# Gate products in pieces of twelve in every second step of a round, in place of six in every step

## The chip, the cores and the metric

The kernel runs on one core of one Trainium2 chip. The metric is the device time of one execution in microseconds (us); the median of the runs shown is used.

## The reference, cut to what matters

The program computes one layer of a hybrid encoder for 2048 frames of width 1024, all in float32:

```python
h = rmsnorm(x)
proj = h @ w_in                       # u | rwkv_in | gate_a | gate_b
o_a = s5_branch(u)                    # diagonal state space model
o_b = rwkv7_branch(rwkv_in)           # 8 heads x 64, delta rule over time
merged = sigmoid(gate_a) * (o_a @ wb[:512]) + sigmoid(gate_b) * (o_b @ wb[512:])
x = x + merged @ w_out
x = x + relu(rmsnorm(x) @ w_ff1)**2 @ w_ff2
return rmsnorm(x)
```

The change concerns the gate columns of `h @ w_in` (2048 columns, here called the gate products) and the RWKV recurrence, since both are computed in the same stage.

## The kernel before, in words

There are four stages. Stage A normalises x, computes the first part of the input projection and the state space branch. Stage B (`phase_b`) runs the RWKV recurrence and, beside it, all the gate products. Stage C merges the branches and applies `w_out`; stage D is the feed-forward part. This case is about stage B.

**The gate products** are made by the generator `gates` (from L957). The outer loop runs over four windows `w` of 512 frames, the inner one over 16 column blocks `m` of 128. One tile `gp` (128 columns by 512 frames, one PSUM bank, two banks in turn) takes eight blocks k of the contraction, and each block takes three TensorE products (`mm3`, L120 to L123: high part by low part, low by high, high by high). So a tile is 24 products of 128x128 by 128x512, and there are 64 tiles and 1536 products. When a tile is done, ScalarE copies it out of PSUM to `gs` (L1015) and a DMA on SP's queue stores it in `gt_d` one tile later (L1016, through `late`). At the start of a tile `loadw` (L965 on) asks for the next block's weights: in the first window ScalarE and GpSimd split raw weights into high and low part (L976, L977), later the parts are read back from `gs_d` (L972). Two weight slots exist, one for even and one for odd m. At the start of each window eight tiles `gh` of the normalised input are loaded from `h_d`, and five steps pass without a product.

**The recurrence** is worked in 16 blocks of 128 frames. For each block there are three generators: `elem` (element-wise preparation, with the products `n` and `bo`), `inv` (the products `m`, `vt`, `kb`, `mv`, a small triangular inverse on VectorE at L813 and L815 that goes through memory by `inv_d` and comes back as `X`, then the products `P`, `D`, `P`, `D` in `levels`), and `chain` (the carried state: product `R`, VectorE add `Rs` at L903, product `U`, ScalarE copy `VU` at L909, products `S` and `y`, VectorE update `SB` at L928; twice per block, then the output norm with the products `var` and `gt`).

**Rounds and steps.** In round i the function `robin` (L82) takes turns: one step of `chain` for block i-2, one step of `gates`, one step of `elem` for block i, one step of `inv` for block i-1. A step is what a generator does up to its next `yield`. `elem` and `inv` last 15 steps and `chain` 10, so that a full round has 15 steps; `gates` is a side generator that goes on from round to round and is run to its end after the last. Four steps make a tile.

**What sets the order.** Engines execute their instructions strictly in the order of their streams. The order in which the Python code calls the instructions is a priority: a planner builds each engine's stream with estimated durations, and where the instruction that is next by priority is not ready by its estimate it puts a later one there that is ready. Instructions marked with `pin` (the products `m`, `mv`, the first `P` and `D`, and `R`) must stay behind the instruction that was called before them on the same engine. The products of one tile stay in their order.

Of the kernel before, what the change touches and what calls it, by code (L numbers as in the profile page):

```python
# [21 lines left out]
NK = DM // 128  # L22
# [97 lines left out]
def mm3(nc, ps, wh, wl, xh, xl, start, stop):  # L120
    nc.tensor.matmul(ps, wh, xl, start=start, stop=False)  # L121
    nc.tensor.matmul(ps, wl, xh, start=False, stop=False)  # L122
    nc.tensor.matmul(ps, wh, xh, start=False, stop=stop)  # L123
# [487 lines left out]
def phase_b(tc, nc, K, io, pm_d, ob_d, h_d, gt_d, gs_d, inv_d):  # L611
    V, A, P, T = nc.vector, nc.scalar, nc.gpsimd, nc.tensor
    NS = S // 128
    with ExitStack() as st:
# [61 lines left out]
        def pin(f):  # L676
            return lambda *a, **k: tc.keep_in_program_order(f(*a, **k))
# [279 lines left out]
        def gates():  # L957
            late, keep = Late(), Late()

            def raww(m, q=nc.sync):  # L960
                wr = (gw, gt)[m % 2].tile([128, NK, 128], F32, tag="wr", name=f"gwr{m}")
                pin(q.dma_start)(wr, io["win"][18 + m])
                return wr

            def loadw(m, wr=None):  # L965

                pool = (gw, gt)[m % 2]
                wh = pool.tile([128, NK, 128], F32R, tag="wh", name=f"gwh{m}")
                wl = pool.tile([128, NK, 128], F32R, tag="wl", name=f"gwl{m}")
                if m >= 16:  # L970
                    for e, t in enumerate((wh, wl)):
                        nc.sync.dma_start(t.bitcast(F32), gs_d[m % 16, e])  # L972
                    return wh, wl
                if wr is None:
                    wr = raww(m)
                A.copy(wh, wr)  # L976
                P.tensor_tensor(wl, wr, wh, op=ALU.subtract)  # L977

                def store():
                    for e, t in enumerate((wh, wl)):  # L980
                        nc.sync.dma_start(gs_d[m, e], t.bitcast(F32))

                keep.put(store)
                return wh, wl

            wr0 = raww(0, nc.gpsimd)
            yield
            wr1 = raww(1)
            for w in range(NW):
                hs = []  # L990
                for k in range(NK):
                    t = (gw if k < 5 else gt).tile([128, 2, 512], F32R, tag=f"h{k}", name=f"gh{w}_{k}")
                    q = nc.sync if w or k >= 5 else nc.gpsimd
                    (q.dma_start if w else pin(q.dma_start))(
                        t.bitcast(F32), h_d[:, w, :, k, :].rearrange("i p t -> p i t"))
                    r = t[:, 0], t[:, 1]
                    hs.append(r)
                if w == 0:
                    nxt = loadw(0, wr0)
                for _ in range(5):  # L1000
                    yield
                for m in range(16):
                    wh, wl = nxt
                    j = 16 * w + m
                    if j == 15:
                        keep.flush()
                    if j + 1 < 16 * NW:
                        nxt = loadw(j + 1, None if j else wr1)
                    pp = psd.tile([128, 512], F32, tag="d", name=f"gp{j}")
                    for k in range(NK):  # L1010
                        mm3(nc, pp, wh[:, k], wl[:, k], hs[k][0], hs[k][1], k == 0, k == NK - 1)
                        if k % 2 and k < NK - 1:
                            yield
                    sg = gt.tile([128, 512], F32, tag="sg", name=f"gs{j}", bufs=2)
                    A.copy(sg, pp)  # L1015
                    late.put(lambda m=m, w=w, sg=sg: nc.sync.dma_start(  # L1016
                        gt_d[128 * m:128 * m + 128, 512 * w:512 * w + 512], sg))
                    yield
            late.flush()

        gg = Side(gates())
        next(gg)
        load(0, nc.gpsimd)
# [867 lines left out]
```

## Time and profile before

| | |
|---|---|
| median of 3 runs | 3067.3 us (3063.57 to 3067.74) |
| the profiled execution | 3067.71 us, its span 3065.8 us |
| mean granted TensorE clock | 0.975 |
| TensorE busy over the span | 95% |
| VectorE, ScalarE, GpSimd busy | 62%, 37%, 40% |
| stage B's gate products | first start 550.2 us, last 1349.0 us |

Times in the trace are counted from the start of the span. A row of the timeline gives the start, the duration, the engine, the line, what is written from what, and in brackets the idle time of the engine before it with what ended it. Matmuls are pipelined, so the distance between two starts says more than the duration. PE is TensorE, PEld its weight loads, DVE VectorE, ACT ScalarE, POOL GpSimd.

### The profile page before, as it was taken

What the parts mean: (1) busy time and instruction counts of PE and PEld (TensorE: products, weight loads), DVE (VectorE), ACT (ScalarE), POOL (GpSimd) and SP (SyncE); (2) the same over time, 40 slices, a digit from 0 to 9 for tenths busy, and PEclk for the clock granted to TensorE, in tenths of its full rate; (3) what the DMA queues carried; (4) which work ended last, traced back from release to release, by engine and by line L of the source; (5) the groups of instructions that cost most, each with busy time, mean ns of one, the idle gap of its engine ahead of it and who ended that gap; (6) DMA issues with size and microseconds to landing.
All of it is one profiled execution on the core that took longest, in us unless ns stands there. A gap on an engine that the chain in (4) does not pass through costs nothing.

```text
span 3065.8 us, 45565 instructions
## 1 busy us (share of the span) xinstructions
PE 2915.4 (95%) x17024; PEld 2329.5 (76%) x17024; DVE 1897.8 (62%) x3307; ACT 1121.4 (37%) x1797; POOL 1234.7 (40%) x1082
## 2 busy tenths in 40 slices
PE   8989999689999999999999989999999999999998
PEld 6757777467777777777878778887788788888886
DVE  6366885467777677535322376658655476666667
ACT  5342111234333333234444365555433432222232
POOL 3101101754443343113333345555544565555563
PEclk9999999789999999999999999999999999999999
DMA  4344444755656455367665653333533486666664
GB/s 154 96 132 148 132 148 133 255 187 176 187 167 207 120 149 181 118 195 229 194 213 166 192 188 124 110 110 114 169 113 107 134 240 151 151 151 151 153 146 148
DMA packets 328172, 486.04 MB, mean 159 GB/s; under 512 B 112832, under 2 KB 171712, under 8 KB 327952
## 3 DMA queue, kind: packets, MB, share of 16 engines
q1 hardware_dynamic: 298352, 438.08, 44.8%
q0 software_dynamic: 12960, 40.87, 7.3%
q10 hardware_dynamic: 16640, 4.20, 0.5%
q8 instruction: 134, 2.20, 0.3%
q14 instruction: 86, 0.70, 0.1%
HBM read 327.71 MB, written 147.85 MB: 155 GB/s over the span
## 4 chain that ended last, share of the span: by engine, by line
PE 55%; DVE 10%; DMA 6%; issue 4%; POOL 3%; ACT 2%; SPq 1%; POOLq 0%; DVEq 0%; ACTq 0%
PE s L121 6%; PE s L122 6%; PE s L123 6%; PE f L121 6%; PE f L123 6%; PE f L122 6%; PE gp L121 2%; PE gp L122 2%; PE gp L123 2%; DMA g<-gt_d 1%; PE o L121 1%; DVE yt L813 1%; PE o L122 1%; DVE YC L815 1%; PE o L123 1%
## 5 line engine op out<-in xcount | busy, mean ns | idle before, releaser
L121 PE MATMUL f<-bl,w1h 128*128 128x512 f32 x896 | 354.4, 396 | 9.4 <-ACT w1h L1378 9.3
L122 PE MATMUL f<-bh,w1l 128*128 128x512 f32 x896 | 350.7, 391 | 5.1 <-POOL w1l L1382 5.1
L123 PE MATMUL f<-bh,w1h 128*128 128x512 f32 x896 | 352.1, 393 | 0.0
L121 PE MATMUL s<-w2l,ah 128*128 128x512 f32 x784 | 305.8, 390 | 2.9 <-ACT s L1619 2.9
L122 PE MATMUL s<-w2h,al 128*128 128x512 f32 x784 | 305.7, 390 | 0.0
L123 PE MATMUL s<-w2h,ah 128*128 128x512 f32 x784 | 305.6, 390 | 0.0
L1382 POOL TENSOR_TENSOR w1l<-w1r,w1h 128x512 fp32r<-128x512 f32 x122 | 179.9, 1478 | 180.2 <-ACT w1h L1378 179.8
L121 PE MATMUL gp<-gh,gwh 128*128 128x512 f32 x512 | 225.8, 441 | 21.4 <-ACT gwh L976 14.9
L122 PE MATMUL gp<-gh,gwl 128*128 128x512 f32 x512 | 211.6, 413 | 12.5 <-POOL gwl L977 11.7
L1378 ACT CAST w1h<-w1r 128x512 fp32r<-128x512 f32 x224 | 137.9, 620 | 207.9 <-PE f L123 149.7
L1596 POOL TENSOR_TENSOR al<-ra,ah 128x1024 fp32r<-128x1024 f32 x64 | 168.4, 2634 | 109.2 <-ACT ah L1595 109.0
L123 PE MATMUL gp<-gh,gwh 128*128 128x512 f32 x512 | 209.3, 409 | 0.0
L1626 DVE TENSOR_TENSOR c<-c,s 128x512 f32<-128x512 f32 x224 | 149.9, 684 | 90.5 <-PE s L123 89.8
L121 PEld LDWEIGHTS f<-bl,w1h 128*128 128x128 f32 x896 | 169.4, 189 | 45.7 <-ACT w1h L1378 10.9
L122 PEld LDWEIGHTS f<-bh,w1l 128*128 128x128 f32 x896 | 169.1, 189 | 44.6 <-POOL w1l L1382 7.9
L123 PEld LDWEIGHTS f<-bh,w1h 128*128 128x128 f32 x896 | 168.9, 188 | 38.3
L121 PE MATMUL p<-hl,wh 128*128 128x512 f32 x448 | 183.1, 409 | 0.2
L122 PE MATMUL p<-hh,wl 128*128 128x512 f32 x448 | 178.7, 399 | 0.0
L123 PE MATMUL p<-hh,wh 128*128 128x512 f32 x448 | 178.2, 398 | 0.0
L121 PEld LDWEIGHTS s<-w2l,ah 128*128 128x128 f32 x784 | 147.5, 188 | 33.9 <-ACT s L1619 3.3
L123 PEld LDWEIGHTS s<-w2h,ah 128*128 128x128 f32 x784 | 147.6, 188 | 30.9
L122 PEld LDWEIGHTS s<-w2h,al 128*128 128x128 f32 x784 | 147.5, 188 | 30.6
(392 smaller groups left out, 6778.7 us busy)
## 6 DMA issues: line engine op xcount, KB each, us to landing
w1r<-in_w_dram SPq DMA_DIRECT2D x64, 512.0 KB, 3.5
r_d<-c SPq DMA_DIRECT2D x128, 256.0 KB, 2.0
ra<-r_d SPq DMA_DIRECT2D x64, 512.0 KB, 3.5
gwl<-gs_d SPq DMA_DIRECT2D x48, 512.0 KB, 4.5
gwh<-gs_d SPq DMA_DIRECT2D x48, 512.0 KB, 4.8
ch<-r_d POOLq DMA_DIRECT2D x42, 512.0 KB, 5.7
gt_d<-gs SPq DMA_DIRECT2D x64, 256.0 KB, 5.0
g<-gt_d SPq DMA_DIRECT2D x64, 256.0 KB, 3.4
```

The source lines that it names most:

```text
L121: nc.tensor.matmul(ps, wh, xl, start=start, stop=False)
L122: nc.tensor.matmul(ps, wl, xh, start=False, stop=False)
L123: nc.tensor.matmul(ps, wh, xh, start=False, stop=stop)
L813: V.tensor_tensor(tv, NC[:, 0:k, k:k + 1].to_broadcast([64, k, n]), YC[:, k:k + 1, k:16].to_broadcast([64, k, n]), op=ALU.mult)
L815: V.tensor_tensor(YC[:, 0:k, k:16], YC[:, 0:k, k:16], tv, op=ALU.add)
L1378: cast = A.copy(h, o)
L1382: (P if n % 2 or edge else V).tensor_tensor(l, o, h, op=ALU.subtract)
L1596: P.tensor_tensor(l, raw[n], h, op=ALU.subtract)
L1626: V.tensor_tensor(d, d, bank, op=ALU.add if i in (4, 5, 6) else ALU.subtract)
```

## The change

A tile's 24 products were called as four pieces of six (two blocks k each), with one step after each. Now they are called as two pieces of twelve (four blocks k each), with two steps after each: the second of the two steps does nothing in `gates`. A tile still lasts four steps and begins in the same step; the number, operands and order of the products within a tile are the same. The blocks k = 2, 3 and k = 6, 7 are called one step earlier than before, and so are the copy at L1015 and what hangs on the end of a tile.

```diff
                     for k in range(NK):
                         mm3(nc, pp, wh[:, k], wl[:, k], hs[k][0], hs[k][1], k == 0, k == NK - 1)
-                        if k % 2 and k < NK - 1:
+                        if k == 3:
+                            yield
                             yield
                     sg = gt.tile([128, 512], F32, tag="sg", name=f"gs{j}", bufs=2)
                     A.copy(sg, pp)
                     late.put(lambda m=m, w=w, sg=sg: nc.sync.dma_start(
                         gt_d[128 * m:128 * m + 128, 512 * w:512 * w + 512], sg))
+                    yield
                     yield
             late.flush()
```

## The prediction

> **What bounds the kernel now.** I read the page's busy table first, then the busy time by stretches of stage B, then who TensorE waited for in that stage, and last the timeline of one undisturbed round.
>
> ```profile
> span 3065.8 us, 45565 instructions
> PE 2915.4 (95%) x17024; PEld 2329.5 (76%) x17024; DVE 1897.8 (62%) x3307; ACT 1121.4 (37%) x1797; POOL 1234.7 (40%) x1082
> L121 PE MATMUL gp<-gh,gwh 128*128 128x512 f32 x512 | 225.8, 441 | 21.4 <-ACT gwh L976 14.9
> ...
> 540.00:600.00 60.00, 32.15 (x117) 23.92 (x115) 28.36 (x35) 14.84 (x24) 47.71 (x66) 0.72 0.77 256
> 600.00:800.00 200.00, 179.56 (x1786) 138.82 (x1787) 143.23 (x258) 71.12 (x118) 97.72 (x106) 0.93 0.61 190
> 800.00:1000.00 200.00, 195.53 (x2019) 153.35 (x2015) 154.10 (x322) 72.70 (x123) 83.18 (x118) 1.00 0.59 179
> 1000.00:1200.00 200.00, 186.01 (x2064) 143.06 (x2062) 135.07 (x274) 66.53 (x117) 72.29 (x101) 0.96 0.53 155
> 1200.00:1310.00 110.00, 105.33 (x1095) 82.93 (x1092) 67.25 (x157) 27.83 (x50) 18.11 (x22) 1.00 0.41 129
> 1310.00:1350.00 40.00, 38.55 (x317) 29.86 (x316) 8.88 (x14) 7.28 (x15) 1.29 (x1) 1.00 0.55 177
> ```
>
> The stretches give, after their length, the busy time of PE, PEld, DVE, ACT and POOL, then the granted clock and the DMA share. TensorE is the bound of stage B: from 600 to 1310 us it is busy for 179.56 + 195.53 + 186.01 + 105.33 = 666.4 of 710 us, and VectorE, the next, for 499.7. From 1310 to 1350 VectorE has hardly any work left while TensorE still is 38.55 of 40 us busy: the last gate products stand there alone. So a microsecond that TensorE saves anywhere in the stage shortens this rest and, as far as stage C starts behind it, the whole. What can be saved is the 43.6 us of idle time, what the lower clock costs (0.07 x 200 + 0.04 x 200, some 22 us), and time inside the busy share.
>
> ```profile
> PE gp L121 <- ACT gwh L976: 14.9, 2, 9.8
> PE P L677 <- DVE X L825: 12.9, 6, 5.1
> PE gp L122 <- POOL gwl L977: 11.7, 3, 9.3
> PE P L871 <- DVE X L865: 4.1, 3, 1.9
> PE U L907 <- DVE Rs L903: 2.5, 6, 0.6
> ```
>
> These rows are TensorE's waits in the stage: us in total, times, the longest. The two on gate weights lie mostly at the stage's start. The wait of `P` is on a matrix that comes back from memory. The wait of `U` is the only one of note in the chain: 2.5 us in 6 of 32 places.
>
> ```profile
> 868.89 1.09 PE L677 MATMUL R<-SB,AG 128*64 128x128 f32 x8
> 869.91 0.50 PE L122 MATMUL gp<-gh,gwl 128*128 128x512 f32 x1
> ...
> 873.43 0.50 PE L121 MATMUL gp<-gh,gwh 128*128 128x512 f32 x1
> ...
> 877.71 0.50 PE L121 MATMUL gp<-gh,gwh 128*128 128x512 f32 x1
> ...
> 878.97 0.39 PE L123 MATMUL gp<-gh,gwh 128*128 128x512 f32 x1
> 879.20 1.05 PE L804 MATMUL vt<-cstb,vm 128*128 128x128 f32 x8
> 880.19 1.09 PE L677 MATMUL R<-SB,AG 128*64 128x128 f32 x8
> 881.20 0.50 PE L121 MATMUL gp<-gh,gwh 128*128 128x512 f32 x1
> 881.54 0.39 PE L122 MATMUL gp<-gh,gwl 128*128 128x512 f32 x1
> 881.77 0.39 PE L123 MATMUL gp<-gh,gwh 128*128 128x512 f32 x1
> ...
> 882.47 0.40 PE L123 MATMUL gp<-gh,gwh 128*128 128x512 f32 x1
> 882.79 1.14 PE L907 MATMUL U<-Rs,Y 64*64 64x64 f32 x16
> 883.86 0.50 PE L121 MATMUL gp<-gh,gwh 128*128 128x512 f32 x1
> ...
> 887.04 0.50 PE L121 MATMUL gp<-gh,gwh 128*128 128x512 f32 x1
> ...
> 890.36 0.79 PE L121 MATMUL gp<-gh,gwh 128*128 128x512 f32 x1
> ...
> 894.30 0.48 PE L121 MATMUL gp<-gh,gwh 128*128 128x512 f32 x1
> ...
> 896.77 0.48 PE L122 MATMUL gp<-gh,gwl 128*128 128x512 f32 x1
> ...
> 898.48 0.40 PE L121 MATMUL gp<-gh,gwh 128*128 128x512 f32 x1
> ...
> 903.23 0.50 PE L121 MATMUL gp<-gh,gwh 128*128 128x512 f32 x1 [0.57 <-DMA gwh<-gs_d]
> ...
> 905.43 0.50 PE L122 MATMUL gp<-gh,gwl 128*128 128x512 f32 x1
> ...
> 908.95 0.50 PE L121 MATMUL gp<-gh,gwh 128*128 128x512 f32 x1
> ...
> 910.53 0.69 PE L881 MATMUL D<-Y,Ps 32*32 32x32 f32 x32
> ```
>
> This is one round, from `R` of its first half at 868.89 to its last `D` at 910.53, some 42 us. Each `gp` row, apart from those at 878.97, 881.54, 881.77 and 882.47, begins a run of gate products after other work: 13 runs. Within a run the products start 0.23 us apart (881.54 to 881.77). The second starts 0.34 us after the first (881.20 to 881.54), and `U` starts 0.32 us after the last (882.47 to 882.79), but `vt` only 0.23 (878.97 to 879.20). So a break costs 0.11 us at its one end and 0.09 or nothing at the other: between 0.11 and 0.20 us. I take the middle, 0.155, since both kinds of successor occur.
>
> **The change part by part.** *Fewer runs.* The products, weight loads, copies and DMAs are the same in number; what can fall is the number of runs. A round of 15 steps holds 7.5 pieces instead of 15. Some pieces must still be cut, because a dependent product isn't ready and the planner puts gate products there:
>
> ```profile
> 881.31 0.68 DVE L903 TENSOR_TENSOR Rs<-R,MV 64x512 f32<-64x512 f32 x1
> ...
> 883.97 0.58 ACT L909 COPY VU<-U 64x512 f32<-64x512 f32 x1 [0.49 <-PE U L907]
> ```
>
> `R` ends at 880.19 + 1.09 = 881.28 and `Rs` at 881.31 + 0.68 = 881.99, so `U` needs 0.71 us of cover behind `R`. `U` ends at 883.93 and `VU` at 884.55: `S` needs 0.62 us. Today every such place has a piece of six, 6 x 0.23 = 1.4 us. After the change, with pieces in odd steps, `R` to `U` of the first half has twelve products, `U` to `S` has the second `m` block between, `R` to `U` of the second half has nothing; with pieces in even steps it is `U` to `S` of the second half that has nothing. So one place in a round lies bare, where the planner will cut the next piece. In `levels` the products `P`, `D`, `P`, `D` depend on each other; I give that one cut more. This makes 7.5 + 2 = 9.5 runs, 3.5 fewer; over 16 rounds 56 runs, at 0.155 us **-8.7 us**. Bounds: -56 x 0.20 = -11.2 with every break dear, and nothing if each piece is cut again as often as now.
>
> *The bare place.* Covered by three or four products of the next piece it costs only what the chip is later than the planner thought. Nearest row: `U` on `Rs`, 2.5 us over 32 places, 0.08 each; 16 x 0.08 = **+1.3 us**. Uncovered it would be 16 x 0.7 = 11.2 us, the upper end; below, nothing.
>
> *Earlier halves.* Half of the products gain one step of priority, and so do the copy to `gs` on ScalarE, the store of `gs` on SP's queue and the release of a weight slot. The copy frees a PSUM bank out of two, and the next tile does not begin before the fourth step, so it gains nothing. On ScalarE the copy, by its shape about as long as `VU`'s 0.58 us, can stand ahead of `VU`, but ScalarE was idle before `VU` (0.49 us above). For SP, only the store moves past loads of the same step; nothing waits for it before stage C. The weight loads may start a step earlier, worth at most the 11.7 + 14.9 us of the rows above, but their long waits (9.8 and 9.3 us) fall into the first 60 us, where raw weights are split and the tile starts are unmoved. I take **0** for all of these; the ends, a loss or gain as large as 5 us, go into the range.
>
> *The clock.* Half clock follows idle stretches:
>
> ```profile
> 624.00:628.00 4.00, 1.38 (x10) 1.22 (x12) 3.85 (x6) 1.25 (x2) 3.25 (x3) 0.84 0.12 27
> 628.00:632.00 4.00, 4.00 (x18) 2.74 (x16) 2.21 (x3) 0.00 (x0) 4.00 (x3) 0.50 0.75 198
> ```
>
> With 1.38 of 4 us busy, the next 4 us ran at clock 0.50, and lost 2 us. A bare place of 0.7 us is far from 2.6 us idle, so I add nothing. The Trainium skill, "TensorE: Matmul & The Clock Gate", Part 1 on the HAM clock gate, says that the clock is halved after an idle window of about 3.4 us; here it fell with less than that. By the rule the steps without gate products are harmless, and the sum stays; by the row several waits close together would cost 2 us each time.
>
> **Sum.** -8.7 + 1.3 = -7.4 us against the profiled execution's own 3067.7 us gives 3060.3; the median of the runs is 0.4 us lower, so I predict **3060 us** (-0.24%). The two terms at their ends alone reach from 3056 (-11.2) to 3079 (nothing saved and +11.2).
>
> **The rivals.** *No effect: the planner cuts again.* It inserts what is ready, and today's pieces are already broken (a run of one product at 894.30, one of eight at 905.43 made of parts of two pieces). If 13 runs remain, nothing is saved and 3067.7 + 1.3 = 3069 us follows, the same as before. Against it: in the round shown, all runs but four are whole pieces or two of them, so program order does shape the stream. The same time would follow if breaks were free. The Trainium skill, same page, section "Step-by-step: what each phase is for", says that TensorE pulls weight loads ahead of running products when they do not conflict; by that rule a break would cost nothing and the sum would be 3069. The trace disagrees for `U` (0.32 against 0.23) and agrees for `vt`.
>
> *Slower: `P` is left waiting.* `P` is pinned, everything on TensorE queues behind it, and its input comes back from memory. Today gate products in every step stand before it, and still it waited 12.9 us in 6 of 16 rounds, 2.15 us each. If twelve are spent at once and the step before `P` is empty, it may be met too early in every round: 16 x 2.15 = 34.4, which is 21.5 us more; less the 8.7 saved and with the 1.3 that makes 3067.7 + 21.5 - 7.4 = 3082 us. Should each wait halve the clock as above, up to 10 x 2 us come on top. It decides from the point where `P`'s waits reach 12.9 + 7.4 = 20 us. For it speaks that the last `D`, which ends the inverse begun with `m` just behind the first `R`, stands at the very end of the round, with no slack behind it; against it that the planner fills by readiness, and that VectorE, not a count of steps, sets when `X` is ready.
>
> *Much faster.* The waits of `P` (12.9 + 4.1) and the clock's 22 us depend on where the pieces happen to fall. If half of that 39 us goes, 3060 - 19.5 = 3041 us. Nothing in the change aims at them, but a new order throws these dice again, in both directions.
>
> **How the numbers follow.** Forecast 0.32, no effect 0.25, slower 0.30, much faster 0.13. A run of this kernel tells about 0.2% (6 us) from no change. Forecast and much faster are faster: 0.45. No effect is the same: 0.25. Slower by `P`: 0.30. The forecast's own range is 3051 (3056 and 5 us of the unknown costs) to 3062, where no change begins. The range over the cases is 3036 to 3090: the lower end takes in half of the dice's gain with the 5 us of unknown costs, the upper end the 3082 with some clock loss.
>
> **What would show it right or wrong.** Fewer runs of gate products per round (9 or 10 instead of 13), and a mean of the `gp` L121 products below 441 ns, would show the first step; the same 13 runs would show the planner's rival. TensorE's wait for `Rs` and for `VU` should stay under 5 us in all; near 11 us the cover was lost. The wait of `P` for `X` above 20 us and a clock under 0.93 in the stretches from 600 to 1200 us would show the slower rival. The last `gp` product should start near 1342 us instead of 1349. If stage B shortens but the time doesn't, stage C's start was bound by its loads.

## The result, and the profile after

The changed kernel took 3148.4 us (median of 4 runs, 3145.3 to 3150.9), the kernel before beside it 3067.5 us. The ratio is 1.0265, with a 95% interval of 1.0247 to 1.0283: 81 us slower, where 7 us faster was forecast. No run falls into the range of 3036 to 3090 us.

The busy table of the changed kernel, and its stretches of stage B (length, then busy PE, PEld, DVE, ACT, POOL, granted clock, DMA share, GB/s):

```profile
span 3143.1 us, 45578 instructions
PE 2927.0 (93%) x17024; PEld 2341.4 (74%) x17024; DVE 1901.2 (60%) x3307; ACT 1121.3 (36%) x1797; POOL 1229.5 (39%) x1082
L121 PE MATMUL gp<-gh,gwh 128*128 128x512 f32 x512 | 223.2, 436 | 38.8 <-ACT gwh L976 23.5
...
600.00:800.00 200.00, 160.86 (x1521) 121.87 (x1521) 127.04 (x240) 62.04 (x101) 86.08 (x93) 0.88 0.54 170
800.00:1000.00 200.00, 191.36 (x2089) 151.39 (x2087) 142.67 (x285) 69.01 (x120) 78.40 (x108) 0.97 0.56 171
1000.00:1200.00 200.00, 175.47 (x1617) 135.09 (x1613) 121.10 (x248) 58.27 (x100) 68.83 (x93) 0.94 0.55 161
1200.00:1400.00 200.00, 182.00 (x1902) 143.31 (x1900) 108.39 (x237) 49.91 (x91) 38.46 (x48) 0.94 0.38 118
1400.00:1440.00 40.00, 17.16 (x145) 14.28 (x146) 14.65 (x23) 11.16 (x18) 1.26 (x1) 0.65 0.43 106
```

TensorE does the same work with more gaps: between 600 and 800 us it is busy for 160.9 of 200 us, where it was 179.6. The waits of TensorE in the stage (us in total, times, longest):

```profile
PE P L677 <- DVE X L825: 29.8, 9, 8.7
PE gp L121 <- ACT gwh L976: 23.5, 5, 9.5
PE g L121 <- ACT wgh L1114: 19.3, 1, 19.3
PE gp L122 <- POOL gwl L977: 17.2, 5, 9.5
...
PE U L907 <- DVE Rs L903: 3.1, 5, 1.1
```

The end of the stage, in the timeline of TensorE of the changed kernel (start, duration, engine, line, product, in brackets the idle time before):

```profile
1380.99 0.39 PE L122 MATMUL gp<-gh,gwl 128*128 128x512 f32 x1
...
1388.18 1.98 PE L677 MATMUL P<-X,TM 64*64 64x64 f32 x32 [6.57 <-DVE X L825]
...
1433.61 0.80 PE L121 MATMUL g<-zl,wgh 128*128 128x512 f32 x1 [19.31 <-ACT wgh L1114]
```

and the first product of stage C in the kernel before:

```profile
1351.77 0.49 PE L121 MATMUL g<-zl,wgh 128*128 128x512 f32 x1 [2.38 <-ACT wgh L1112]
```

SP's queue, first the kernel before and then the changed one: the store of the recurrence's last block, and behind it the loads of stage C:

```profile
1337.84 0.37 SPq L953 DMA_DIRECT2D ob_d<-ys  x1
...
1344.01 1.59 SPq L1090 DMA_DIRECT2D zt<-z_d  x2
...
1421.49 0.38 SPq L953 DMA_DIRECT2D ob_d<-ys  x1
1423.93 3.20 SPq L1092 DMA_DIRECT2D zt<-z_d  x4
```

Stage C begins 81.8 us later; the two executions differ by 77.3 us in all, so the whole loss lies ahead of stage C. Before, the recurrence's last product on TensorE ended at 1333 us and gate products ran on until 1349. Now the gate products are used up at 1381 us and the recurrence goes on alone until 1414; stage C's loads stand behind its last store. The stage is no longer bound by TensorE's work but by the length of the recurrence's rounds. The tail alone also shows the clock: behind 6.57 us of idle time `P` takes 1.98 us, at a granted clock of 0.50 from 1388 to 1392 us, where it takes 1.15 below, at full clock. That agrees with the Trainium skill, "TensorE: Matmul & The Clock Gate", Part 1 on the HAM clock gate, by which an idle window of about 3.4 us halves the clock.

**Where a round got longer.** From the timelines I took the way of one round: from the end of `m`'s masking `TM` (L785) over memory to the first `yt` (L813), the 30 small operations of the inverse (L813, L815), over memory to `X` (L825), to `P`, to the end of the last `D`, and to the next `TM`. The sums over the stage, in us, worked out from the starts and durations of these rows (16 blocks; 15 gaps for the last column, counted as negative where the next `TM` ends ahead of the last `D`):

| | `TM` to `yt` | inverse | to `X` | to `P` | `P` to last `D` | last `D` to next `TM` |
|---|---|---|---|---|---|---|
| before | 165.4 | 200.5 | 154.5 | 14.1 | 160.3 | 18.0 |
| after | 129.6 | 233.2 | 153.8 | 13.7 | 159.8 | 108.7 |

The mean distance of two rounds goes from 45.0 to 50.8 us (15 rounds, 675.0 and 761.6 us between the first and the last `yt`). Two things stand out. The last column rises from 18.0 to 108.7 us; before, it was negative in 5 of 15 rounds, which means that both halves of the next `m` were through before the last block's `D`. Of these 90.7 us the first column takes back 35.8, which leaves some 55. And the inverse itself takes 14.6 us in place of 12.5, some 33 us in all. The other three columns stay within 1 us.

*The first.* The timeline of TensorE before, in a round of the negative kind, without the gate products between:

```profile
1220.71 1.16 PE L677 MATMUL m<-AR,BK 64*128 64x128 f32 x14 [0.91 <-DVE bv L757]
1223.38 1.16 PE L677 MATMUL m<-AR,BK 64*128 64x128 f32 x16
...
1227.99 1.15 PE L677 MATMUL P<-X,TM 64*64 64x64 f32 x32 [0.94 <-DVE X L825]
...
1235.19 0.69 PE L881 MATMUL D<-Y,Ps 32*32 32x32 f32 x30
1235.81 1.09 PE L677 MATMUL R<-SB,AG 128*64 128x128 f32 x8
```

and after, in the round at about the same place:

```profile
1204.18 0.94 PE L881 MATMUL D<-Y,Ps 32*32 32x32 f32 x32
1205.05 1.09 PE L677 MATMUL R<-SB,AG 128*64 128x128 f32 x8
1206.07 1.16 PE L677 MATMUL m<-AR,BK 64*128 64x128 f32 x16
1207.16 1.14 PE L907 MATMUL U<-Rs,Y 64*64 64x64 f32 x16
1208.66 0.48 PE L677 MATMUL m<-AR,BK 64*128 64x128 f32 x2
```

Before, both halves of the next `m` (1220.71, 1223.38) stand ahead of this round's `P` and `D`, and the way of the next inverse through memory has begun. After, one half stands behind `R` and the other behind `U`. The cause is in the code: the first `m` of each half is pinned behind the instruction that was called last on TensorE. In the order of calls `chain` comes first, then `gates`, `elem`, `inv`. With a piece in every step, that last instruction is a gate product, which waits for nothing of the recurrence. In a step without a piece it is the chain's `R` (first half of the block) or `U` (second half); `R` stands behind the last `D`, and so the next inverse can't begin before this one has ended. This is called the bond below. Of two neighbouring steps one is empty, so one half is always bound. In the streams, the second half's `m` stands ahead of the last `D` in 5 of 15 rounds before, in none after.

*The second.* VectorE in the changed kernel:

```profile
1220.02 0.17 DVE L813 TENSOR_TENSOR yt<-NC,YC 64x15 f32<-64x15 f32 x1
...
1224.91 0.21 DVE L813 TENSOR_TENSOR yt<-NC,YC 64x60 f32<-64x60 f32 x1
1225.06 1.74 DVE L939 RECIPROCAL y<-y 128x256 f32<-128x256 f32 x1
1226.72 0.15 DVE L815 TENSOR_TENSOR YC<-YC,yt 64x60 f32<-64x60 f32 x1
1226.79 1.73 DVE L941 RECIPROCAL y<-y 128x256 f32<-128x256 f32 x1
1228.45 0.14 DVE L813 TENSOR_TENSOR yt<-NC,YC 64x55 f32<-64x55 f32 x1
...
1230.88 1.76 DVE L736 RECIPROCAL sq<-n 128x256 f32<-128x256 f32 x1
...
1235.58 0.15 DVE L815 TENSOR_TENSOR YC<-YC,yt 64x15 f32<-64x15 f32 x1
```

Each of the 30 small operations waits for the one before, and between them the planner has put what was ready: reciprocals of 1.7 us between operations of 0.2 us. This inverse lasts from 1220.02 to 1235.73, 15.7 us; its fastest round before, undisturbed but for one operation, took 7.6.

### The profile page after: what moved, and what is told of

Its sections match the earlier page's. It is cut to its first block, busy times and chain, and to the rows that moved or that the text cites. A ratio compares the mean times of both kernels' runs of the same rounds, so it can differ in the third digit from the quotient of the medians.

```text
span 3143.1 us, 45578 instructions
## 1 busy us (share of the span) xinstructions
PE 2927.0 (93%) x17024; PEld 2341.4 (74%) x17024; DVE 1901.2 (60%) x3307; ACT 1121.3 (36%) x1797; POOL 1229.5 (39%) x1082
## 4 chain that ended last, share of the span: by engine, by line
PE 52%; DVE 12%; DMA 8%; issue 4%; POOL 3%; ACT 2%; SPq 1%; DVEq 0%; POOLq 0%; ACTq 0%
PE f L121 6%; PE f L123 6%; PE f L122 6%; PE s L122 5%; PE s L121 5%; PE s L123 5%; DMA g<-gt_d 3%; PE gp L121 2%; PE gp L122 2%; PE gp L123 2%; DVE yt L813 2%; DVE YC L815 1%; DMA wor<-in_wout_dram 1%; PE m L677 1%; PE o L121 1%
## 5 line engine op out<-in xcount | busy, mean ns | idle before, releaser
L121 PE MATMUL f<-bl,w1h 128*128 128x512 f32 x896 | 354.9, 396 | 6.6 <-ACT w1h L1380 6.6
L121 PE MATMUL s<-w2l,ah 128*128 128x512 f32 x784 | 305.1, 389 | 0.4 <-ACT s L1621 0.4
L121 PE MATMUL gp<-gh,gwh 128*128 128x512 f32 x512 | 223.2, 436 | 38.8 <-ACT gwh L976 23.5
L122 PE MATMUL gp<-gh,gwl 128*128 128x512 f32 x512 | 214.6, 419 | 19.4 <-POOL gwl L977 17.2
L1380 ACT CAST w1h<-w1r 128x512 fp32r<-128x512 f32 x224 | 137.9, 620 | 207.9 <-PE f L123 154.5
L121 PEld LDWEIGHTS f<-bl,w1h 128*128 128x128 f32 x896 | 169.5, 189 | 42.5 <-ACT w1h L1380 7.7
L121 PE MATMUL p<-hl,wh 128*128 128x512 f32 x448 | 182.5, 407 | 0.2
L121 PEld LDWEIGHTS s<-w2l,ah 128*128 128x128 f32 x784 | 147.2, 188 | 31.2 <-ACT s L1621 0.8
## 6 DMA issues: line engine op xcount, KB each, us to landing
r_d<-c SPq DMA_DIRECT2D x128, 256.0 KB, 2.0
gt_d<-gs SPq DMA_DIRECT2D x64, 256.0 KB, 4.7
g<-gt_d SPq DMA_DIRECT2D x64, 256.0 KB, 3.4
```

The lines of the kernel that those rows point to most:

```text
L1380: cast = A.copy(h, o)
```

## The experiments

Three theories. **Anchor**: the loss comes from what `m` is pinned behind. **Cover**: the steps without gate products bare the chain's waits, as the prediction feared. **VectorE**: the planner's other order stretches the small inverse, whatever `m` does. All times below are medians beside runs of the kernel before on the same chip; sums are those of the table, from one profiled execution each.

### Pieces of 11, 1, 11, 1 (e1)

```diff
-                        mm3(nc, pp, wh[:, k], wl[:, k], hs[k][0], hs[k][1], k == 0, k == NK - 1)
-                        if k == 3:
-                            yield
-                            yield
+                        if k % 4 < 3:
+                            mm3(nc, pp, wh[:, k], wl[:, k], hs[k][0], hs[k][1], k == 0, False)
+                            continue
+                        T.matmul(pp, wh[:, k], hs[k][1], start=False, stop=False)
+                        T.matmul(pp, wl[:, k], hs[k][0], start=False, stop=False)
+                        yield
+                        T.matmul(pp, wh[:, k], hs[k][0], start=False, stop=k == NK - 1)
+                        if k == 3:
+                            yield
...
                         gt_d[128 * m:128 * m + 128, 512 * w:512 * w + 512], sg))
                     yield
-                    yield
```

> The changed kernel with the last product of each twelve left over for the empty step: pieces of 11, 1, 11, 1. The lumps are nearly the same, but in every step the first product m of the inverse again stands behind a gate product and not behind the chain's R or U. Anchor theory (m is pinned behind R or U where a step has no gate product, so the next inverse can't begin before the last one has ended): 3060 to 3090 us, some m of the second half ahead of the last D again. Cover theory (steps without gate products bare the chain's waits): as the changed kernel, 3140 to 3150 us. VectorE theory (the planner's other order on VectorE stretches the small inverse at L813 and L815, whatever m does): no clear step, 3110 to 3150 us.

(The edit is against the changed kernel.) 3082.0 us, ratio to before 1.0074 (1.0049 to 1.0098). One product out of twelve, left in the otherwise empty step, takes back some 62 of the 81 us. The second half's `m` stands ahead of the last `D` in 4 rounds again. The lumps are nearly as large as in the changed kernel, so the cover theory falls.

### Before, with m tied behind the chain (e2, e7)

```diff
+        last = {}
+        def behind(ins, n):
+            if n in last:
+                tc.add_manual_dep(ins.ins, last[n].ins.name, mybir.DependencyInfo(
+                    mybir.DependencyClass.NoSync, mybir.DependencyReason.DATA), reason=f"behind {n}")
+            return ins
...
-                        pin(T.matmul)(mps[e][:, o:o + 128], BK[er, h, 2 * c:2 * c + 2, :], AR[er, h, :, tc_],
-                                      start=True, stop=True)
+                        mm = pin(T.matmul)(mps[e][:, o:o + 128], BK[er, h, 2 * c:2 * c + 2, :], AR[er, h, :, tc_],
+                                           start=True, stop=True)
+                        if c and h == 0 and e == 0:
+                            behind(mm, "U")
...
-                    T.matmul(up[uc, 64 * h:64 * h + 64], Y[uc, h, :], R[uc, 64 * h:64 * h + 64],
+                    last["U"] = T.matmul(up[uc, 64 * h:64 * h + 64], Y[uc, h, :], R[uc, 64 * h:64 * h + 64],
                              start=True, stop=True)
```

> The kernel before, pieces of six in every step, with one order added: the first product m of a block's second half stays behind the chain's U of that round. Anchor theory: slower by most of the change's loss, 3115 to 3160 us. Cover theory: nothing was uncovered, 3060 to 3075 us. VectorE theory: 3060 to 3100 us, as its order falls.

3134.5 us, ratio 1.0239 (1.0221 to 1.0257): 71 us slower with all pieces of six in place. The same was done with the first half and `R` (`if not c and h == 0 and e == 0: behind(mm, "R")`):

> The kernel before, pieces of six, with the first product m of a block's first half kept behind the chain's R of that round: the other of the two anchors that an empty step gives. No m can then stand ahead of the last D in any round. Anchor theory: 3115 to 3160 us. Cover theory: 3060 to 3075 us.

3143.8 us, ratio 1.0255 (1.0232 to 1.0277). Either bond alone makes the loss of the change, without the change. In both kernels the inverse got longer too, 256.0 us with `U` and 220.7 with `R` in place of 200.5, and the last column of the table went to 96.9 and 124.7: the runs show what a bond brings with it in all, not what it would cost with the inverse as it was.

### After, with m pinned behind the last gate product (e3)

```diff
-                        mm3(nc, pp, wh[:, k], wl[:, k], hs[k][0], hs[k][1], k == 0, k == NK - 1)
+                        last["g"] = mm3(nc, pp, wh[:, k], wl[:, k], hs[k][0], hs[k][1], k == 0, k == NK - 1)
...
+                        mq = T.matmul if h == 0 and e == 0 else pin(T.matmul)
+                        mm = mq(mps[e][:, o:o + 128], BK[er, h, 2 * c:2 * c + 2, :], AR[er, h, :, tc_],
+                                start=True, stop=True)
+                        if h == 0 and e == 0:
+                            behind(mm, "g")
```

(`mm3` returns its last product here.)

> The changed kernel, pieces of twelve and empty steps, where the first product m of each half is pinned behind the gate product called last, in whatever step, and not behind whatever was called last on TensorE. Anchor theory: 3055 to 3090 us. Cover theory: 3140 to 3150 us, since the empty steps are all there. VectorE theory: 3110 to 3150 us.

3077.5 us, ratio 1.0058 (1.0040 to 1.0076): 67 of the 81 us are back, with all the empty steps. A round of this kernel, TensorE, gate products left out (its lines are some ten further on):

```profile
1096.70 0.94 PE L677 MATMUL m<-AR,BK 64*128 64x128 f32 x13
1099.80 0.49 PE L791 MATMUL m<-AR,BK 64*128 64x128 f32 x2 [1.03 <-DVE TM L796]
1100.88 1.16 PE L677 MATMUL m<-AR,BK 64*128 64x128 f32 x14
1103.56 1.15 PE L677 MATMUL P<-X,TM 64*64 64x64 f32 x32
...
1110.97 0.69 PE L892 MATMUL D<-Y,Ps 32*32 32x32 f32 x30
1111.59 1.09 PE L677 MATMUL R<-SB,AG 128*64 128x128 f32 x8
```

Both halves of `m` are ahead of `P` again.

### After, with the reciprocals behind the small inverse (e4)

```diff
-            V.reciprocal(fl(sq)[:, 0:256], np_[:, 0:256])
+            behind(V.reciprocal(fl(sq)[:, 0:256], np_[:, 0:256]), "Y")
...
-            V.reciprocal(y2[:, 0:256], y2[:, 0:256])
+            behind(V.reciprocal(y2[:, 0:256], y2[:, 0:256]), "Y")
...
-                V.tensor_tensor(YC[:, 0:k, k:16], YC[:, 0:k, k:16], tv, op=ALU.add)
+                last["Y"] = V.tensor_tensor(YC[:, 0:k, k:16], YC[:, 0:k, k:16], tv, op=ALU.add)
```

(and the second halves, L738 and L941, in the same way)

> The changed kernel, where the reciprocals of VectorE (L736, L738, L939, L941) stay behind the small inverse at L813 and L815 of the same round. VectorE theory: the inverse takes 8.5 to 10 us in place of 14.6 on the mean, some 5 us in each of 16 rounds, so 3065 to 3090 us. Anchor theory: the rounds stay strung together and keep that loss; what the shorter inverse gives comes on top of it, since it lies on the same path: 3080 to 3125 us. Cover theory: 3140 to 3150 us.

3075.4 us, ratio 1.0039 (1.0021 to 1.0057). The inverse sums to 152.1 us in place of 233.2, the way from the last `D` to the next `TM` stays long (112.8 us), and `m`'s second half is ahead of the last `D` in no round. So the bond is still there, and yet the loss is nearly gone. VectorE in this kernel:

```profile
1130.58 0.19 DVE L823 TENSOR_TENSOR YC<-YC,yt 64x39 f32<-64x39 f32 x1
1130.80 0.18 DVE L821 TENSOR_TENSOR yt<-NC,YC 64x28 f32<-64x28 f32 x1
1131.01 0.18 DVE L823 TENSOR_TENSOR YC<-YC,yt 64x28 f32<-64x28 f32 x1
1131.23 0.17 DVE L821 TENSOR_TENSOR yt<-NC,YC 64x15 f32<-64x15 f32 x1
1131.43 0.17 DVE L823 TENSOR_TENSOR YC<-YC,yt 64x15 f32<-64x15 f32 x1
1131.52 1.74 DVE L947 RECIPROCAL y<-y 128x256 f32<-128x256 f32 x1
```

The reciprocals come behind the last `YC`. My expectation of the anchor theory, that the bond keeps its loss and only the stretch is given back (3080 to 3125 us), was too high, and the VectorE theory's range was met. But that theory had the stretch come "whatever `m` does", and the runs contradict this: with `m` bound and the reciprocals free to go between, the inverse sums to 220.7 to 256.0 us (the changed kernel, e2, e7 and e11 below); with `m` not bound to the chain, to 200.5 to 209.3 (the kernel before, e1, e3 and e8 below). Bond and stretch lie on one path, and what counts is whether that path is longer than TensorE's own work in a round. Either remedy brings it down to about there.

### Both remedies, and the kernel before with them (e6, e5, e9, e8)

> The changed kernel with both: m pinned behind the last gate product, and the reciprocals behind the small inverse. If the two act on one path and each of them alone has already brought the rounds down to TensorE's own work, no more than the better of the two: 3060 to 3080 us. If they add, 3010 to 3050 us.

3068.2 us, ratio 1.0019 (0.9997 to 1.0040): the changed kernel with both can't be told from the kernel before. They don't add.

> The kernel before, with the reciprocals of VectorE kept behind the small inverse of the same round as in e4_after_recip. If the small inverse lies on the path that sets the length of a round even where m is free, 3030 to 3055 us; if rounds of this kernel are bound by TensorE's own work, as the prediction said, no change: 3058 to 3070 us.

3063.4 us, ratio 0.9993 (0.9977 to 1.0008). The inverse falls from 200.5 to 155.0 us here too, and the time doesn't move: what the inverse gains turns up as a longer way from the last `D` to the next `TM`, 101.8 us in place of 18.0. With `m` behind the gate products, the inverse isn't what sets the length of a round.

> The kernel before, where the first product m of each half isn't pinned at all (the planner puts it where it is ready) and the reciprocals stay behind the small inverse. If more freedom for m shortens the rounds further, below e5_before_recip: 3020 to 3050 us; if TensorE's own work is the floor, 3055 to 3070 us.

3059.3 us, ratio 0.9996 (0.9980 to 1.0011): nothing either.

> The kernel before, where the first product m of each half isn't pinned at all. It shuffles the planner's order about as much as e2_before_tied and e7_before_m0_tied do, but binds nothing to the chain. Anchor theory: 3055 to 3080 us. If any shuffle of the order costs some 70 us, as a rival has it, 3110 to 3150 us.

(In these two, the first `m` of each half is called with `T.matmul` in place of `pin(T.matmul)`.) 3057.3 us, ratio 0.9984 (0.9974 to 0.9994). A new order that binds nothing does no harm. The gain of 0.16% is below what counts as a change here, though its interval lies below 1; it is the best of the kernels tried.

### Whole tiles at once (e11, e10)

The `yield`s at k = 3 are left out and four stand at the end of a tile: pieces of 24 in every fourth step.

> Pieces of 24 in every fourth step and nothing else changed. Anchor theory: in three of four steps m has no gate product before it; since one bound half is enough to string the rounds together, the loss doesn't grow with the piece: 3130 to 3160 us. Cover theory: the bare places double or triple, 3180 to 3300 us.

3150.1 us, ratio 1.0285 (1.0270 to 1.0301). This is 89 us over the kernel before, in place of 81, with intervals that overlap: three empty steps of four cost hardly more than one of two. The loss is that of the bond, with the longer inverse that comes with it, and not of the bared places.

> Whole tiles: pieces of 24 gate products in every fourth step, three empty steps between, with m pinned behind the last gate product and the reciprocals behind the small inverse as in e6_after_free_recip. If empty steps as such cost nothing once the two bonds are loose, 3055 to 3080 us; cover theory: above 3090 us; if fewer runs of gate products save 0.155 us each, as the prediction had it, about 6 us under e6_after_free_recip for its 10 fewer runs per stage and fuller pieces, 3055 to 3068 us.

3069.1 us, ratio 1.0024 (1.0010 to 1.0038): with the bonds loosened, even pieces of 24 cost only 8 us.

## Why the prediction was wrong

**What bounds the stage: right before, wrong after.** That TensorE's own work is the bound of the kernel before is borne out: a shorter inverse left its time as it was (e5, e9). But the margin was never worked out. The prediction took it that from 1310 us on the last gate products "stand there alone"; in fact the last block's chain ran on TensorE until 1333 us. Its result was stored at 1337.84, 13.9 us ahead of stage C's first product, and in the changed kernel, with no gate product left, these two are 12.1 us apart, in e3 10.4. So the recurrence could have ended only some 2 to 4 us later before stage C felt it; this is an estimate from these rows. It ended 81 us later, with rounds 5.8 us longer. The prediction did see that the last `D` stands at the very end of a round "with no slack behind it".

**The step that failed** is "Fewer runs", in its walk through the steps. It says of pieces in odd steps that "`U` to `S` has the second `m` block between", and so took `m` there as cover for the chain. It did not see that `m` is pinned, and that with no gate product in the step it is pinned behind `U` or `R`. The list of pinned products ahead of the prediction has `m`, but the prediction works with the pin of `P` alone. The term that is missing from the sum is the bond: 71 us with `U` (e2) or 82 us with `R` (e7), in the kernel that is otherwise that of before, the longer inverse that came with it included.

**Runs of gate products.** They fell in the stream from 225 to 185, 40 in place of the 56 forecast, and the mean of the `gp` L121 products fell from 441 to 436 ns, a sign that the prediction had asked for. (In the round that it shows, five of the 13 runs are neither a whole piece nor two of them, not four; nothing in the sum hangs on it.) A saving of 0.155 us each was not seen in the time: e6 with 197 runs took 6.4 us more than before, and its interval leaves room for no more than 1 us less. Whether a break costs what the starts say and something else takes it back, or whether it costs nothing, no run here tells apart.

**The bare place.** Right. `U` waited 3.1 us for `Rs` and the products behind `VU` 1.4 us, together under the 5 us that the prediction allowed; e6 and e10, with the bonds loose, lie 6 and 8 us over the kernel before, and the interval of e6 takes in no change.

**Earlier halves and the clock, taken as 0.** The waits on gate weights rose from 14.9 + 11.7 to 23.5 + 17.2 us, 14 us more, over the 5 us that were allowed. The clock fell to 0.88 in 600 to 800 us, from 0.93. Both go mostly with the bond and not with the pieces: with pieces of six and the bond the waits are 33.3 us (e2) and 35.0 us (e7) and the clock 0.84 and 0.85, with pieces of twelve and `m` free the waits are 27.7 us and the clock 0.90 (e3).

**The rivals.** "Slower: `P` is left waiting" had the right side and a sign that did show, `P`'s waits of 29.8 us, above its point of 20. But its mechanism, gate products spent too early, is not the cause: `P` waits 23.9 and 26.5 us in e2 and e7 too, with pieces of six in every step, and in the kernel with whole tiles and loose bonds (e10) the pieces come in larger lumps still, and it takes 3069 us. Its price of 3082 also missed the result. "No effect" and "much faster" did not come. The range missed because all its cases shared one premise, that only waits inside the rounds could change and not what may overlap with what.

**Open.** The 11 and 1 pieces and the freed `m` keep 14 to 19 us over the kernel before. The inverse sums to 202.4 and 209.3 us there, little above before, and from `X` to `P` it is 18.6 and 19.0 in place of 14.1 us; where the rest comes from was not followed up. Behind stage C's first product the profiled executions lasted from 1700 to 1714 us, so that differences of this size between totals are only in part the stage's: in that of e5 stage C began 8 us later than in that of the kernel before, and the time is the same.

## What to carry to other kernels

An order that is stated relative to "whatever came last" can be changed by any edit that moves what comes last: before thinning out a filler, look for pins that stand on it. Where a planner may overlap two rounds, ask of a change not only what it adds to each wait but which instruction of the next round it lets begin; and give the bound its margin, how much longer the second longest path may grow before it takes over. In a chain of very short dependent operations a planner can do harm by filling gaps, here with 1.7 us between operations of 0.2 us; whether it costs anything depends on that margin.

## What the runs showed of the hardware

I had not expected that the clock can stay up through steps without the large products. A stretch of the kernel before, at the start of a window of frames, where only small products of the recurrence run behind one gate product at 783.98 (columns as in the stretches above):

```profile
784.00:788.00 4.00, 3.77 (x65) 3.11 (x63) 0.69 (x1) 1.31 (x3) 0.00 (x0) 1.00 1.10 297
```

TensorE counts as busy for 3.77 of 4 us and the clock stays at 1.00. It fell to 0.50 after the 2.6 us of idle time quoted in the prediction, which were not one gap but mainly two, of 0.92 and 1.81 us with two products `m` between, and after the 6.57 us above. Once down, it didn't come back with small products that had gaps between them. In the tail of the changed kernel:

```profile
1388.00:1392.00 4.00, 3.14 (x52) 2.95 (x54) 0.12 (x1) 0.58 (x1) 0.00 (x0) 0.50 0.00 0
1392.00:1396.00 4.00, 2.05 (x50) 1.76 (x46) 1.44 (x2) 0.26 (x1) 0.00 (x0) 0.50 0.02 4
1396.00:1400.00 4.00, 3.27 (x40) 2.67 (x40) 0.39 (x1) 1.19 (x4) 0.00 (x0) 0.50 0.00 0
1400.00:1404.00 4.00, 2.88 (x34) 2.72 (x36) 0.30 (x1) 0.58 (x1) 0.00 (x0) 0.50 0.00 0
1404.00:1408.00 4.00, 3.58 (x44) 3.39 (x40) 1.43 (x3) 0.00 (x0) 0.00 (x0) 0.54 0.02 4
1408.00:1412.00 4.00, 2.29 (x46) 2.02 (x46) 0.09 (x1) 1.44 (x3) 0.00 (x0) 1.00 0.00 0
```

With 2.05 to 3.27 of each 4 us busy it stayed at 0.50 for 16 us; it rose behind the stretch with 3.58.
